# Gate rows split into single jobs, a reordered opening and final norm, and projection sums laid 384 + 256 over two banks

## The chip, the cores and the metric

The kernel runs on one core of one Trainium2 chip, in one launch. The metric is device time in microseconds (us); lower is better. Five engines work side by side, each on its own queue of instructions: TensorE (PE, matmuls), VectorE (DVE), ScalarE (ACT), GpSimd (POOL) and SyncE (SP, whose queue issues nearly all transfers here).

## What is computed

Two layers over 128 context tokens and 512 latent tokens. Each layer has a mixer and a SwiGLU feed-forward part; both take a normalised input with shift and scale, and are added to x through a gate. Shift, scale and gate come from one small vector-matrix product per layer; the context tokens have a conditioning vector of their own.

```python
def rms_norm(x, g):
    return x * lax.rsqrt(jnp.mean(x * x, axis=-1, keepdims=True) + EPS) * g

for l in range(2):                       # for the context with c_ctx, for the latents with c
    sh1, sc1, g1, sh2, sc2, g2 = jnp.split(jax.nn.silu(cvec) @ w_ada[l] + b_ada[l], 6, axis=-1)
    h = rms_norm(x, norm_g[l, 0]) * (1 + sc1) + sh1
    y = even_mixer(h) if l % 2 == 0 else attention(h)    # pooling and short convolution; grouped-query attention
    x = x + g1 * y
    h = rms_norm(x, norm_g[l, 1]) * (1 + sc2) + sh2
    a, b = jnp.split(h @ w_ffn_in[l], 2, axis=-1)
    x = x + g2 * ((jax.nn.silu(a) * b) @ w_ffn_out[l])
y = rms_norm(x, final_g)
```

Here `D_MODEL` is 1024 and `D_FF` 2816. The keys and values of the context are outputs too.

## The kernel before

x stays in SBUF transposed: 128 partitions by 8 blocks of channels by 640 tokens, the context first (0 to 127), the latents behind (128 to 639). All matmuls are fp32 in accuracy: each operand is split into a high and a low half, and three products (high by high, high by low, low by high; `THREE`) are summed. The names show it: `wh_in` and `wl_in` are the halves of in-projection weights loaded as `raw_in`, `ah` and `al` those of x times the scale. The high half of a weight is made on ScalarE (L144), the low half on DVE (L145).

One output block of a projection is a PSUM tile of two banks of 512 columns; `block_mm` (L282) lays tokens 0 to 319 in the first bank and 320 to 639 in the second (`HT` is 320), so each weight is used by a pair of 320-wide matmuls. `project` runs the blocks of one projection; its `each(i)` is called ahead of block i, its `done` after it, one step late. `residual` (L515) adds a block to x with the gate: three operations through `update` (L501), for the context, for 192 latents in the first bank and for 320 in the second.

The rows of shifts, scales and gates, 96 of 128 outputs each, come from two places. The parts needed first are computed by PE at the start (`ada_pe`, `ada_row`, `ada_turn`: a product per quarter of a chunk, a copy on ScalarE, a transposition by PE). All others are computed on DVE by `AdaDve`: one row is a 512 KB transfer on SP's queue (L354), four reductions of 128 x 512 (L371) and four reads of their sums. `ada.run(n)` computes the next n rows of a list of jobs; a job (layer, first row, count) is written to `mod` only when its last row is done. The numbers in the `each` and `fast_each` arguments thus set how much of DVE's time goes to rows at which step.

The program runs in this order (times from the profile): the opening, up to 62.8 us, in an order written out by hand (`manual_schedule`); behind it a scheduler orders each engine's instructions, where the reductions of the rows stay in the order of the program. In-projection of layer 0, 13 blocks (`pi`), to 166; its output projection (`po`) to 223; the feed-forward part of layer 0 in three groups, each with its up-projection and a down-projection: group 0 has four plain blocks and, from 285, four by the fast algorithm (`fast_blocks`, which forms sums of weights on DVE, L236 to L242, and halves of the SwiGLU product in `uv`, L652 and L657), down-projection `fo0_0` 337 to 394; group 1 fast 394 to 496 and `fo0_1` to 553; group 2 to 672. Then layer 1: attention to 916, plain blocks to 965, fast blocks of group 0 to 1027, `fo1_0` to 1084, and so on, to the final norm.

The final norm (`last1`) works in two parts of 384 and 256 tokens. Sums of squares are multiplied by ones on PE (`ms_fin`), `Norm.finish` makes `rstd` in three steps on ScalarE and three on DVE (L474 to L476), and `out` (L1443) multiplies eight blocks by `rstd`, every third on GpSimd, with a transfer for each two blocks.

Of the kernel before, what the change touches and what calls it, by code (L numbers as in the profile page):

```python
# [36 lines left out]
EARLY = 30  # L37
# [23 lines left out]
def hybrid_step(  # L61
# [611 lines left out]
    def ffn(l, xin, hid, each=None, last=None, spare=None, fast_each=None):  # L673
# [37 lines left out]
        for gi, (f0, f1) in enumerate(GROUPS):  # L711
# [21 lines left out]
            if plain:  # L733
                project(f"fi{l}_{gi}", xin, KB, 2 * plain, in_done, ext=True, each=each and (lambda i: each(i, True)))
# [11 lines left out]
    with tc.tile_pool(name="pool1", bufs=1) as p1:  # L746
# [6 lines left out]
        def ada_load(ch):  # L753
# [851 lines left out]
```

## Time and profile before

| | |
|---|---|
| median of 3 runs | 1377.84 us (1377.27 to 1378.74) |
| profiled execution, its own time | 1376.99 us |
| its span | 1375.2 us |
| PE busy | 1327.7 us, 97% |
| DVE busy | 1081.2 us, 79% |
| ScalarE, GpSimd busy | 636.3 us, 70.3 us |
| mean rate of the transfers | 113 GB/s |

All rows below come from the profiled execution, whose time is 0.85 us under the median; times in them count from the start of its span. L is a line of the kernel before. In a timeline a run of like instructions stands as one row, with the start of its first, the time until its last one ends and their count; idle time ahead of it and what ended it stand in brackets. In a row of windows the columns after the length are the busy time of PE, PE's loads of weights, DVE, ScalarE and GpSimd, each with its number of instructions, then the mean granted clock of PE (1.00 is the 2.4 GHz level, 0.50 the 1.2 GHz one), the mean busy share of the 16 DMA engines and GB/s.

### The profile page before, as it was taken

To read this page: it belongs to the slowest core of one execution; us is meant where nothing else is said; L and a number is where in the kernel's file an instruction comes from. 1 tells how busy PE (TensorE), PEld (TensorE's weight loads), DVE (VectorE), ACT (ScalarE), POOL (GpSimd) and SP (SyncE) were. 2 spreads that over 40 slices of the span, in tenths; PEclk is the share of its full clock that TensorE was granted. 3 is DMA by queue.
4 is the path that set the end of the run, shared out by engine and by line. 5 is a ranking of instruction groups with operands and counts; after the bars stand their busy time and mean duration, and the time that the engine had idled before them with its cause. 6 is when DMAs were issued, how large, how long until landed. Compare 5 with 4: busy or idle time off the path is not lost.

```text
span 1375.2 us, 22538 instructions
## 1 busy us (share of the span) xinstructions
PE 1327.7 (97%) x8929; PEld 1294.1 (94%) x8929; DVE 1081.2 (79%) x2182; ACT 636.3 (46%) x1155; POOL 70.3 (5%) x73
## 2 busy tenths in 40 slices
PE   6989999989999999999999999999999999999995
PEld 3889999989999999999998899999999999999995
DVE  4899988999988898789976777689993577446745
ACT  3532335744135531454565675477551255314543
POOL 3200000000000000000013121000000000000013
PEclk7999999999999999999999999999999999999998
DMA  9635523134533254324531110031242122311212
GB/s 363 250 117 176 195 93 123 64 106 169 172 123 114 95 187 154 108 92 140 188 95 55 43 49 34 32 134 53 106 154 77 62 76 78 123 62 62 77 47 77
DMA packets 36872, 155.54 MB, mean 113 GB/s; under 512 B 4000, under 2 KB 11168, under 8 KB 26016
## 3 DMA queue, kind: packets, MB, share of 16 engines
q1 hardware_dynamic: 36768, 154.12, 32.2%
q8 instruction: 70, 1.15, 0.3%
q14 instruction: 34, 0.28, 0.1%
HBM read 148.60 MB, written 2.88 MB: 110 GB/s over the span
## 4 chain that ended last, share of the span: by engine, by line
PE 77%; DVE 16%; ACT 3%; issue 2%; DMA 1%; SPq 0%; POOL 0%; DVEq 0%; ACTq 0%; POOLq 0%
PE fi L630 24%; PE fo L289 21%; PE fi L289 7%; PE pq L289 5%; PE pi L289 5%; DVE junk L371 5%; PE po L289 4%; DVE wl_fi_p L145 3%; PE wb L289 2%; PE wa L289 2%; PE o L1326 2%; PE s L1276 1%; PE t L1309 1%; ACT wh_fi_p L144 1%; DMA raw_ada<-wada 1%
## 5 line engine op out<-in xcount | busy, mean ns | idle before, releaser
L144 ACT ACTIVATE wh_fi_p<-raw_fi 128x512 fp32r<-128x512 f32 x252 | 153.9, 626 | 219.5 <-PE fi L630 108.6
L371 DVE CUSTOM_DVE_ANT_0 junk<-rawa,silb 128x512 f32<-128x512 f32 x336 | 237.0, 705 | 6.5 <-DMA rawa<-wada 2.2
L145 DVE TENSOR_TENSOR wl_fi_p<-raw_fi,wh_fi_p 128x512 fp32r<-128x512 f32 x252 | 170.1, 686 | 64.1 <-ACT wh_fi_p L144 63.9
L506 DVE SCALAR_TENSOR_TENSOR x<-fo,mod,x 128x128 f32<-128x128 f32 (+1 forms) x144 | 55.5, 433 | 94.1 <-PE fo L289 90.8
L144 ACT ACTIVATE wh_fo<-raw_fo 128x1024 fp32r<-128x1024 f32 (+1 forms) x48 | 47.5, 990 | 145.4 <-PE fo L289 121.2
L630 PE MATMUL fi<-bh,wh_fi_p 128*128 128x320 f32 x288 | 89.0, 309 | 0.7 <-DVE x L506 0.5
L630 PE MATMUL fi<-bh,wl_fi_p 128*128 128x320 f32 x288 | 88.9, 309 | 0.6 <-DVE wl_fi_p L145 0.6
L630 PE MATMUL fi<-ah,wl_fi_p 128*128 128x320 f32 x288 | 88.8, 308 | 0.0
L630 PE MATMUL fi<-al,wh_fi_p 128*128 128x320 f32 x288 | 88.7, 308 | 0.0
L630 PE MATMUL fi<-ah,wh_fi_p 128*128 128x320 f32 x288 | 88.4, 307 | 0.0
L630 PE MATMUL fi<-bl,wh_fi_p 128*128 128x320 f32 x288 | 88.4, 307 | 0.0
L289 PE MATMUL fo<-al,wh_fo 128*128 128x320 f32 x352 | 80.8, 310 | 0.0
L289 PE MATMUL fo<-ah,wh_fo 128*128 128x320 f32 x352 | 80.6, 310 | 0.1
L289 PE MATMUL fo<-ah,wl_fo 128*128 128x320 f32 x352 | 80.4, 309 | 0.0
L289 PE MATMUL fo<-bh,wh_fo 128*128 128x320 f32 x328 | 75.2, 310 | 0.0
L289 PE MATMUL fo<-bh,wl_fo 128*128 128x320 f32 x328 | 75.0, 310 | 0.0
L289 PE MATMUL fo<-bl,wh_fo 128*128 128x320 f32 x328 | 74.9, 310 | 0.0
L630 PE MATMUL fi<-x0h,wh_fi_p 128*128 128x320 f32 x216 | 69.0, 323 | 5.0 <-DVE uv L652 3.6
L630 PE MATMUL fi<-xh,wh_fi_p 128*128 128x320 f32 x216 | 68.0, 320 | 2.6 <-DVE uv L652 2.1
L630 PE MATMUL fi<-x0l,wh_fi_p 128*128 128x320 f32 x216 | 66.9, 311 | 0.0
L630 PE MATMUL fi<-x0h,wl_fi_p 128*128 128x320 f32 x216 | 66.9, 311 | 0.0
L289 PE MATMUL pi<-ah,wh_in 128*128 128x320 f32 (+1 forms) x256 | 62.3, 326 | 4.7 <-ACT ev L526 3.8
(375 smaller groups left out, 3808.7 us busy)
## 6 DMA issues: line engine op xcount, KB each, us to landing
raw_fi<-wfi SPq DMA_DIRECT2D x44, 1024.0 KB, 4.8
rawa<-wada SPq DMA_DIRECT2D x84, 512.0 KB, 3.4
raw_fo<-wfo SPq DMA_DIRECT2D x16, 1024.0 KB, 4.9
raw_ada<-wada SPq DMA_DIRECT2D x12, 512.0 KB, 9.9
raw_in<-win SPq DMA_DIRECT2D x6, 1024.0 KB, 6.4
raw_fo<-wfo SPq DMA_DIRECT2D x8, 768.0 KB, 4.2
raw_qkv<-wqkv SPq DMA_DIRECT2D x6, 1024.0 KB, 5.0
raw_out<-wout SPq DMA_DIRECT2D x4, 1024.0 KB, 4.8
```

Of the source, the lines that this page charges most:

```text
L144: S.activation(h, src, AF.Copy)
L145: eng.tensor_tensor(out=l, in0=src, in1=h.bitcast(F32), op=ALU.subtract)
L289: PE.matmul(ps[:, h, 0 : hi - lo], w[a][:, k, cols], rhs[b][:, k0 + k, lo:hi], start=k == 0 and a == b, stop=k == kn - 1 and a == 1,)
L371: op = V.tensor_tensor_reduce(out=self.junk, in0=raw[:, cols], in1=self.silb[:, c, cols], scale=1.0, scalar=0.0, op0=ALU.mult, op1=ALU.add ...
L506: V.scalar_tensor_tensor(out=xs, in0=got[:, 0 : b - a], scalar=mod[l][:, gate0 + m, c : c + 1], in1=xs, op0=ALU.mult, op1=ALU.add,)
L630: PE.matmul(out, w[a][:, k, :], ops.get(OPERAND[p], b)[:, k, :], start=fresh and k == 0 and a == b, stop=k == ops.kn - 1 and a == 1, skip_ ...
L1276: PE.matmul(self.ps[:, hf, 0:HT], bufB[a][:, self.h, q0 : q0 + P], kt[b][:, self.kv, hf * HT : hf * HT + HT], start=n == 0, stop=n == 2,)
L1309: PE.transpose(flat(pt)[:, s * P : s * P + P], self.pe[:, s * P : s * P + P], ident)
L1326: PE.matmul(po[:, 0 : 2 * P], vt[a][:, self.kv, s * P : s * P + P], got[b][:, s, :], start=s == 0 and n == 0, stop=s == 4 and n == 2,)
```

## The change

- **Layout.** Sums for `po`, `fo`, `wa` and `wb` (all that go into x) are cut at token 384 instead of 320 (`CUT`). All latents then lie as 256 columns in each bank, and one operation of 128 x 2 x 256 updates them; the context has one of its own. The in-projections keep 320.
- **Gate rows.** The feed-forward gates of both layers are eight jobs of one row each, so that a residual needs its own gate row alone. Rows that DVE computes move: the opening keeps 4; `pi` has 16 instead of 18 (per step 1,1,1,1,1,2,2,2,1,1,1,1,1 instead of 2,2,2,2,2,2,2,1,1,1,1,0,0); `po` and the two blocks ahead of it keep theirs; the plain blocks of layer 0 have 0 instead of 3, its fast blocks 0, 8 and 6 in the three groups instead of 4, 4 and 3, its down-projections 12, 14 and 8 instead of 12, 12 and 8. In layer 1 eight rows go from the fast blocks of group 0 to `fo1_0`, one a step; the transfers of the first two start at the head of the stage.
- **Opening.** The first weights are loaded ahead of chunk 3; 6, 3 and 14 matmuls on zeros are put in (`turn_over`); the transposition of chunk 2 no longer stands behind a part of chunk 3; squares of x move from GpSimd to ScalarE and their sums to DVE; the order of splits and matmuls changes.
- **Final norm.** The first part's `finish` gets a high priority; the multiplications by `rstd` are four operations of four blocks each on DVE, none on GpSimd, with four transfers instead of eight. In DVE's order the second part's finish still stands behind both of the first part's operations.

```diff
-EARLY = 30
+EARLY = 28
...
-    def block_mm(ps, w, rhs, kn, ext=False, mcol=0, k0=0, ks=None):
+    CUT = CTX + LAT // 2
+
+    def block_mm(ps, w, rhs, kn, ext=False, mcol=0, k0=0, ks=None, cut=HT):
...
-        span = ((0, 0, HT), (1, HT, TX if ext else T))
+        span = ((0, 0, cut), (1, cut, TX if ext else T))
...
     def residual(ps, m, l, gate0):
-        parts = ((0, 0, CTX, ps[:, 0]), (1, CTX, HT, ps[:, 0, CTX:]), (1, HT, T, ps[:, 1]))
-        update(m, l, gate0, parts)
+        update(m, l, gate0, [(0, 0, CTX, ps[:, 0])])
+        xs = halves(x[:, m, CTX:T])
+        V.scalar_tensor_tensor(
+            out=xs,
+            in0=flat(ps)[:, CTX : CTX + 768].rearrange("p (a b) -> p a b", a=2)[:, :, 0 : LAT // 2],
+            scalar=mod[l][:, gate0 + m, 1:2],
+            in1=xs,
+            op0=ALU.mult,
+            op1=ALU.add,
+        )
...
-            [(0, 4, 4)] + [(0, 8 * p, 8) for p in (2, 4, 3, 5)] + [(1, 8 * p, 8) for p in (1, 0, 2, 4, 3)]
+            [(0, 4, 4)]
+            + [(0, 8 * p, 8) for p in (2, 4, 3)]
+            + [(0, 40 + b, 1) for b in range(8)]
+            + [(1, 8 * p, 8) for p in (1, 0, 2, 4, 3)]
...
+        ws.load(1, cut=True)
         ada_load(3)
-        ws.load(1, cut=True)
...
+        idle = first[2][:, 0, :]
+
+        def turn_over(n):
+
+            for _ in range(n):
+                PE.matmul(idle, zeror, zeror2, start=True, stop=True)
+
+        turn_over(6)
         acc = {ch: ada_acc(ch) for ch in (2, 3)}
         ada_pe(2, acc[2], range(4))
         row = ada_row(2, acc[2])
-        ada_pe(3, acc[3], range(1))
+        turn_over(3)
         ada_turn(2, row)
-        ada_pe(3, acc[3], range(1, 4))
+        turn_over(14)
         for k in range(4):
-            nrm.add(k, pool_only=True)
-        prep(0, bufA, 0, 0)
-        prep(1, bufA, 0, 0)
-        prep(2, bufA, 0, 0)
-        ws.split(0, ahead=False)
+            prep(k, bufA, 0, 0)
+            if k == 1:
+                ws.split(0, ahead=False)
+        ws.split(1, ahead=False)
+        for k in range(4):
+            nrm.square(k)
+        first_mm(0, range(4))
+        ada_pe(3, acc[3], range(4))
         row = ada_row(3, acc[3])
-        prep(3, bufA, 0, 0)
-        ws.split(1, ahead=False)
-        first_mm(0, range(0, 2))
+        nrm.add_square(V)
...
+        first_mm(1, range(2))
         ada_turn(3, row)
-        first_mm(0, range(2, 4))
-        first_mm(1, range(4))
+        first_mm(1, range(2, 4))
...
-        ada.run(2, hold=False)
+        ada.run(1, hold=False)
+        nrm.add_square(V)
...
+        ada.run(1, hold=False)
...
-            each=lambda i: ada.run(1 + (i < 7) - (i >= 11)),
+            each=lambda i: ada.run(1 + (5 <= i < 8)),
...
-                each=lambda i, plain=False: ada.run(int(i >= 5) if plain else 1 + i % 2),
-                fast_each=lambda gi, n, p: ada.run(int(p == 6 and (gi == 0 or n % 2))),
+                each=lambda i, gi, plain=False: ada.run(0 if plain else 1 + (i % 2 if gi == 0 else int(i > 1))),
+                fast_each=lambda gi, n, p: ada.run(int(p == 6 and gi > 0)),
...
-                (G if k % 3 == 1 else V).tensor_tensor(out=xs, in0=xs, in1=rstd[:, cols], op=ALU.mult)
...
+            V.tensor_tensor(
+                out=xs, in0=xs, in1=rstd[:, None, cols].broadcast_to((P, ks.stop - ks.start, n)), op=ALU.mult
+            )
+            nc.sync.dma_start(yT[:, ks, cols], xs)
...
-            nrm.finish((lo, hi), None)
+            with tc.high_priority():
+                nrm.finish((lo, hi), None)
...
-    gates = AdaDve([(1, 40, 8)], 76)
+    gates = AdaDve([(1, 40 + b, 1) for b in range(8)], 76)
     gates.home(p3, p3, 2, ps_small("junk1"), silb)
+    gates.load()
+    gates.load()
...
-        fast_each=lambda gi, n, p: gates.run(int(gi == 0 and p in (1, 6))),
+        each=lambda i, gi, plain=False: gates.run(0 if plain or gi else 1),
```

How instructions move is shown at three places. On PE in the opening, before (`adap` is a product of a chunk, one row of two matmuls a quarter, `adat` the transposition, `pi_152` the first block of the in-projection):

```order
L306 MATMUL adap_155<-raw_ada_3_103,silc 2x512 x2
L306 MATMUL adap_157<-raw_ada_0_107,silc 2x512 x2
L330 MATMUL adat_171<-kc,row_167 128x2 x4
L306 MATMUL adap_157<-raw_ada_1_109,silc 2x512 x2
L306 MATMUL adap_157<-raw_ada_2_111,silc 2x512 x2
L306 MATMUL adap_157<-raw_ada_3_113,silc 2x512 x2
L289 MATMUL pi_152<-ah,wh_in_0_204 128x320 x2
L289 MATMUL pi_152<-al,wh_in_0_204 128x320 x2
L289 MATMUL pi_152<-ah,wl_in_0_205 128x320 x2
```

and after:

```order
L309 MATMUL adap_161<-raw_ada_3_103,silc 2x512 x2
L827 MATMUL pi_154<-zeror 128x512 x3
L333 MATMUL adat_178<-kc,row_173 128x2 x4
L827 MATMUL pi_154<-zeror 128x512 x14
L292 MATMUL pi_152<-ah,wh_in_0_207 128x320 x2
L292 MATMUL pi_152<-al,wh_in_0_207 128x320 x2
L292 MATMUL pi_152<-ah,wl_in_0_208 128x320 x2
```

The transposition of chunk 2 stood behind a quarter of chunk 3; now matmuls on zeros (`pi_154<-zeror`) stand around it, and all of chunk 3 comes after the first block's matmuls with the first half of x.

On DVE in the in-projection, before, around one of the scaled projections `ev` (`pl` is a pooling result, `junk,got` a reduction of a row, `got` alone the read of its sum):

```order
L915 SCALAR_TENSOR_TENSOR pl_747<-s_4_588,up_578 128x128
L371 ISA junk,got_16_591<-rawa_371,silb 128x512
L371 ISA got_16_591 128x1
L915 SCALAR_TENSOR_TENSOR pl_747<-s_4_588,up_578 128x512
L371 ISA junk,got_16_591<-rawa_371,silb 128x512
L371 ISA got_16_591 128x1
L521 TENSOR_TENSOR ev_754<-pi_676,rstd 128x640
L371 ISA junk,got_16_591<-rawa_379,silb 128x512
L371 ISA got_16_591 128x1
L145 TENSOR_TENSOR bl<-pl_747,bh 128x640
```

and after:

```order
L956 SCALAR_TENSOR_TENSOR pl_760<-s_4_613,up_603 128x128
L956 SCALAR_TENSOR_TENSOR pl_760<-s_4_613,up_603 128x512
L534 TENSOR_TENSOR ev_767<-pi_695,rstd 128x640
L374 ISA junk,got_16_616<-rawa_396,silb 128x512
L374 ISA got_16_616 128x1
L145 TENSOR_TENSOR bl<-pl_760,bh 128x640
L374 ISA junk,got_16_616<-rawa_396,silb 128x512
L374 ISA got_16_616 128x1
```

Two reductions, and their reads, have left the place between `pl` and `ev`.

On DVE where the second down-projection of layer 0 passes into the third group's fast blocks, before (`fo_1_7` is the last block, `wl_fi_16_p` and on are low halves of the fast blocks' weights):

```order
L506 SCALAR_TENSOR_TENSOR x<-fo_1_7_5294,mod_77,x 128x128
L371 ISA junk,got_32_5162<-rawa_5241,silb 128x512
L371 ISA got_32_5162 128x1
L506 SCALAR_TENSOR_TENSOR x<-fo_1_7_5294,mod_77,x 128x192
L371 ISA junk,got_32_5162<-rawa_5241,silb 128x512
L371 ISA got_32_5162 128x1
L506 SCALAR_TENSOR_TENSOR x<-fo_1_7_5294,mod_77,x 128x320
L145 TENSOR_TENSOR wl_fi_16_p_5400<-raw_fi_16_4964,wh_fi_16_p_5399 128x512
L145 TENSOR_TENSOR wl_fi_16_p_5400<-raw_fi_17_5096,wh_fi_16_p_5399 128x512
L236 TENSOR_TENSOR raw_fi_17_5096<-raw_fi_17_5096 128x4x128
```

and after:

```order
L509 SCALAR_TENSOR_TENSOR x<-fo_1_7_5298,mod_77,x 128x128
L374 ISA junk,got_32_5307<-rawa_5246,silb 128x512
L374 ISA got_32_5307 128x1
L523 SCALAR_TENSOR_TENSOR x<-fo_1_7_5298,mod_77,x 128x512
L374 ISA junk,got_32_5307<-rawa_5246,silb 128x512
L374 ISA got_32_5307 128x1
L145 TENSOR_TENSOR wl_fi_16_p_5404<-raw_fi_16_4953,wh_fi_16_p_5403 128x512
L374 ISA junk,got_32_5307<-rawa_5246,silb 128x512
L374 ISA got_32_5307 128x1
L145 TENSOR_TENSOR wl_fi_16_p_5404<-raw_fi_17_5092,wh_fi_16_p_5403 128x512
L374 ISA junk,got_32_5307<-rawa_5246,silb 128x512
L374 ISA got_32_5307 128x1
```

The update of x has one operation less, and reductions now stand between the update and the low halves as well as between these; before, the first ones behind the update came after thirteen other instructions.

## Rows read from the trace of the kernel before

**Rows 1.** The page: busy time by engine; the chain that ended last.

```profile
PE 1327.7 (97%) x8929; PEld 1294.1 (94%) x8929; DVE 1081.2 (79%) x2182; ACT 636.3 (46%) x1155; POOL 70.3 (5%) x73
...
PE 77%; DVE 16%; ACT 3%; issue 2%; DMA 1%; SPq 0%; POOL 0%; DVEq 0%; ACTq 0%; POOLq 0%
```

**Rows 2.** Waits of PE: line, released by, total us, times, longest us.

```profile
PE fi L630 <- DVE uv L652: 5.8, 3, 3.6
PE pi L289 <- DVE wl_in L145: 4.7, 3, 3.4
PE pi L289 <- ACT ev L526: 3.8, 1, 3.8
```

**Rows 3.** Windows: from:to, length, busy us by engine (x instructions), clock, DMA.

```profile
26.00:28.00 2.00, 1.87 (x7) 1.87 (x8) 2.00 (x4) 0.00 (x0) 0.00 (x0) 0.50 1.02 410
75.00:100.00 25.00, 21.24 (x125) 20.79 (x123) 25.00 (x65) 9.00 (x15) 0.33 (x6) 0.86 0.31 106
285.00:300.00 15.00, 10.59 (x60) 9.82 (x59) 15.00 (x33) 5.36 (x11) 0.00 (x0) 0.89 0.26 81
400.00:625.00 225.00, 223.10 (x1490) 218.21 (x1490) 191.56 (x384) 93.34 (x178) 0.00 (x0) 1.00 0.36 123
500.00:550.00 50.00, 50.00 (x340) 50.00 (x339) 45.15 (x113) 7.73 (x9) 0.00 (x0) 1.00 0.47 158
975.00:1025.00 50.00, 47.52 (x318) 46.15 (x318) 50.00 (x114) 24.75 (x47) 0.00 (x0) 1.00 0.37 127
1025.00:1075.00 50.00, 50.00 (x341) 49.96 (x340) 22.26 (x37) 9.37 (x12) 0.00 (x0) 1.00 0.30 106
```

**Rows 4.** Timeline of the start: start us, us, engine, line, operands, xcount [idle].

```profile
10.68 0.60 ACT L324 ACTIVATE row<-adap 98x512 f32<-98x512 f32 x1 [7.79 <-PE adap L306]
...
13.16 1.25 POOL L436 TENSOR_TENSOR ssq_a<-x 128x640 f32<-128x640 f32 x1 [11.27 <-DMA x<-xT]
...
14.43 1.03 PE L306 MATMUL adap<-raw_ada,silc 128*2 128x512 f32 x4 [3.80 <-DMA raw_ada<-wada]
...
17.73 7.21 DVE L485 SCALAR_TENSOR_TENSOR al<-x,sc,ah 128x128 fp32r<-128x128 f32 x6 [0.47 <-ACT ah L483]
...
24.86 1.21 DVE L145 TENSOR_TENSOR wl_in<-raw_in,wh_in 128x1024 fp32r<-128x1024 f32 x1
...
26.13 0.90 PE L289 MATMUL pi<-ah,wl_in 128*128 128x320 f32 x2 [3.42 <-DVE wl_in L145]
...
36.89 8.03 POOL L440 TENSOR_TENSOR ssq_a<-ssq_a,sq_a 128x640 f32<-128x640 f32 x4 [13.42 <-ACT sq_a L438]
...
37.61 1.94 DVE L371 CUSTOM_DVE_ANT_0 junk<-rawa,silb 128x512 f32<-128x512 f32 x1
...
54.14 0.48 DVE L474 SCALAR_TENSOR_TENSOR ssq_a<-ms_a,ssq_a 128x320 f32<-128x320 f32 x1
```

**Rows 5.** The page's costliest groups: xcount | busy us, mean ns | idle before.

```profile
L371 DVE CUSTOM_DVE_ANT_0 junk<-rawa,silb 128x512 f32<-128x512 f32 x336 | 237.0, 705 | 6.5 <-DMA rawa<-wada 2.2
```

**Rows 6.** Timeline, layer 0's second down-projection: one residual's three updates.

```profile
524.60 1.13 DVE L506 SCALAR_TENSOR_TENSOR x<-fo,mod,x 128x128 f32<-128x128 f32 x3
```

**Rows 7.** Chain of waits, layer 0's first down-projection: start us, us, what.

```profile
337.54 56.54 PE fo L289 x384
```

**Rows 8.** Timeline of PE near the end: matmuls of 384 and 256 columns.

```profile
1348.51 0.34 PE L1461 MATMUL fo<-bh,wh_fo 128*128 128x384 f32 x1
...
1354.80 0.28 PE L1461 MATMUL fo<-bh,wh_fo 128*128 128x256 f32 x1
...
1356.81 0.28 PE L1461 MATMUL fo<-bh,wl_fo 128*128 128x256 f32 x1
```

**Rows 9.** Timeline of the tail: final normalisation on DVE.

```profile
1362.17 4.83 DVE L1446 TENSOR_TENSOR x<-x,rstd 128x384 f32<-128x384 f32 x5
...
1366.92 0.41 DVE L474 SCALAR_TENSOR_TENSOR ssq_fin<-ms_fin,ssq_fin 128x256 f32<-128x256 f32 x1
...
1368.15 3.35 DVE L1446 TENSOR_TENSOR x<-x,rstd 128x256 f32<-128x256 f32 x5
```

More of the change, by code (lines that the diff above doesn't have):

```diff
@@ L501, in update @@
     def update(m, l, gate0, parts):
-        assert (l, gate0 // 8, 8) in known
+        assert any((l, gate0 // 8, n) in known for n in range(m + 1, 9))
         for c, a, b, got in parts:
@@ L559, in project @@
                 each(i)
-            pipe.step(lambda: block_mm(ps, w, rhs, kn, ext=ext), lambda: done(i, ps))
+            pipe.step(lambda: block_mm(ps, w, rhs, kn, ext=ext, cut=cut), lambda: done(i, ps))
     def updater(l, gate0, nrm, then):
@@ L733, in ffn @@
             if plain:
-                project(f"fi{l}_{gi}", xin, KB, 2 * plain, in_done, ext=True, each=each and (lambda i: each(i, True)))
+                project(f"fi{l}_{gi}", xin, KB, 2 * plain, in_done, ext=True, each=each and (lambda i: each(i, gi, True)))
             if l in FAST:
@@ L739, in ffn @@
             if gi < len(GROUPS) - 1:
-                project(f"fo{l}_{gi}", hid, f1 - f0, KB, lambda k, ps: residual(ps, k, l, 40), each=each)
+                project(
+                    f"fo{l}_{gi}",
+                    hid,
+                    f1 - f0,
+                    KB,
+                    lambda k, ps: residual(ps, k, l, 40),
+                    each=each and (lambda i: each(i, gi)),
+                )
             else:
@@ L1415, in hybrid_step @@
         for m in range(2):
-            pipe.step(lambda: block_mm(fw[m], wpart[0], bufB, 4, mcol=m, k0=4, ks=range(3)))
+            pipe.step(lambda: block_mm(fw[m], wpart[0], bufB, 4, mcol=m, k0=4, ks=range(3), cut=CUT))
         assert not pipe.due
@@ L1419, in hybrid_step @@
         for m in range(2):
-            pipe.step(lambda: block_mm(fw[m], wpart[0], bufB, 4, mcol=m, k0=4, ks=(3,)), lambda: out_done(m, fw[m]))
+            pipe.step(lambda: block_mm(fw[m], wpart[0], bufB, 4, mcol=m, k0=4, ks=(3,), cut=CUT), lambda: out_done(m, fw[m]))
         for m in range(2, KB):
@@ L1441, in whole, with out @@
             gain(k)
-        def out(cols, step):
-            for k in range(KB):
-                xs = x[:, k, cols]
-                (G if k % 3 == 1 else V).tensor_tensor(out=xs, in0=xs, in1=rstd[:, cols], op=ALU.mult)
-                if k % step == step - 1:
-                    ks = slice(k + 1 - step, k + 1)
-                    nc.sync.dma_start(yT[:, ks, cols], x[:, ks, cols])
+        def out(ks, cols):
+            n = cols.stop - cols.start
+            xs = x[:, ks, cols]
+            V.tensor_tensor(
+                out=xs, in0=xs, in1=rstd[:, None, cols].broadcast_to((P, ks.stop - ks.start, n)), op=ALU.mult
+            )
+            nc.sync.dma_start(yT[:, ks, cols], xs)
         project("fo1_2", bufA, kn, KB - 2, whole)
@@ L1470, in last1 @@
                 nrm.add(KB - 2 + m, V, cols)
-            nrm.finish((lo, hi), None)
+            with tc.high_priority():
+                nrm.finish((lo, hi), None)
             for m in range(2):
                 gain(KB - 2 + m, cols)
-        for h, (lo, hi) in enumerate(spans):
-            out(slice(lo, hi), 2)
+            if not h:
+                out(slice(0, 4), cols)
+        for h, ks in ((0, slice(4, 8)), (1, slice(0, 4)), (1, slice(4, 8))):
+            out(ks, slice(*spans[h]))
     whole_b = tuple(t.rearrange("p a b -> p (a b)") for t in bufB)
```

18 lines of the change are left out of this document (13 added, 5 removed).

## The prediction

> **What bounds the kernel now.** I read the page first: TensorE (PE) is busy for 1327.7 of 1375.2 us, 97%, and the chain that ended last runs through PE for 77% and through VectorE (DVE) for 16% of the span [rows 1]. So at most some 47 us stand idle, and work taken off DVE pays only where PE waits for it. Next I read what PE waited for [rows 2]: the two halves of a SwiGLU product (`uv`), the low halves of the in-projection's weights (`wl_in`) and one scaled projection (`ev`). Each of these hangs on an instruction in DVE's queue. Then the windows around these waits [rows 3]. In 75 to 100 us DVE is busy for all 25.00 us and PE has 125 matmuls; a matmul costs 147 ns at full speed (below), so 170 would fit and 6.6 us are lost, part of it as a gap, part since the granted clock averages 0.86 there: PE waited and then ran some 7 us at the 1.2 GHz level. In 285 to 300 DVE is again busy throughout, 60 matmuls stand where 100 would fit: 6.0 us lost, at a mean clock of 0.89. In 975 to 1025, DVE at 50.00 of 50, PE is idle for 2.5 us and the clock stays at 1.00. In 500 to 550 DVE is at 90% and PE never stops. So a full DVE stalls PE and a DVE at 90% does not; the change takes rows (`AdaDve.run`, four reductions each) out of three full places and puts them into emptier ones.
>
> **The start, -5.5 us (3 to 7).** The first matmul that needs a low half waits 3.42 us, until 26.13, for `wl_in`, which DVE starts only at 24.86 [rows 4]. Two things delay it. PE stands 3.80 us for the fourth-part transfers of chunk 3 and runs them from 14.43, while the transposition of chunk 2, whose input ScalarE has ready at 10.68 + 0.60 = 11.28, is queued behind; the change puts it ahead, and the first scaling can start when x is there, which GpSimd reads from 13.16: some 3.5 us earlier. And DVE's six `al` operations from 17.73 take 7.21 us beside GpSimd's squares; after the change ScalarE squares and only four `al` precede `wl_in`. Worked through, `wl_in` starts at 17 to 18 instead of 24.86, its limit being ScalarE's `wh_in` behind four `ah`. Much of the 7 us is lost again: PE runs these matmuls at the 1.2 GHz level (clock 0.50 in 26 to 28, [rows 3]), the second half of x comes behind the same transfers, and chunk 3 lands later since the first weights now pass it on SP's queue. The second place is the row reductions: one takes 1.94 us from 37.61 while GpSimd's additions run from 36.89 for 8.03 us [rows 4], against 0.705 on average over all 336. Four such lose 4 x 1.23 = 4.9 us on DVE, on the path to the third block's `wl_in` and the norm's step at 54.14. The change puts the additions on DVE itself: a 320-wide two-input operation takes 0.48 and a 256-wide 0.41 [rows 4, 9], so 1.1 ns a column and 0.13 fixed, 0.83 for 640 columns; four cost 3.3 back, and this gives 1.6; three more stand ahead of the second `al` and are covered by PE's queue of matmuls. I get the step at 54.14 to 47.5 to 51 and take 5.5; 3 if the transfers set it, 7 if everything shifts. The extra matmuls on zeros lie where PE was idle; whether they hold the 2.4 GHz level no row shows, so I count no gain. Fourteen of 512 columns, at twice the 0.147 us per 320, take 6.6 us and would end near 19, a loss of 1 to 2 that the 3 contains; at the fast level they end before `wl_in`.
>
> **The in-projection, -5.0 (3 to 6.6).** Five of the first five steps' rows go and three come back later, net two. A row is 4 x 0.705 = 2.8 us [rows 5], taken as 3.0 with the reads of its four sums, so 15 us of DVE leave ahead of the gap in 75 to 100, which should close it and the slow clock behind it: 6.6 at most. But the rows that come back land in a stage where DVE has little room, so over the whole stage only the two rows' 6 us are free. I take 5.0.
>
> **First fast blocks of layer 0, -5.5 (4 to 6).** Four rows leave these blocks and three the plain ones ahead: 20.6 us of DVE in a place that lost 6.0. The wait for `uv` of 3.6 us [rows 2] goes with them; late next would be ScalarE, whose busy time there is 5.36 of 15. **First fast blocks of layer 1, -2.0 (1.2 to 2.4):** eight rows leave, the loss was 2.5. They go into the down-projection behind, where DVE has 22.26 of 50 [rows 3]; seven rows make it 43, below the 90% that cost nothing. The fourteen added small additions (each less than the 0.41 us of a 256-wide operation) lie in the same slack and in that of layer 0's first down-projection; a residual waits for its own gate alone, on one queue.
>
> **The rows put into layer 0's later blocks, +4 (0 to +9).** Nine rows, 27 us, enter 400 to 625, where DVE has 191.56 of 225 [rows 3]: 218.6, or 97%. At 90% the cost was nothing. At 100% it was 2.5 in 50 us, and 225 such us would lose 11.2, less the 1.9 that are idle there already: 9.3. 97% lies nearer the full end, but the place is full only by count and not in arrears; two rows a step, in the second down-projection, make 2 x 3.0 + 1.2 for the split of weights (1.21 for 1024 columns, [rows 4]) + 1.0 for the updates = 8.2 us of DVE in a step of 7.07, and the overhang slides into the next blocks, as the order shows. I take 4. Their transfers, 512 KB each on SP's queue, enter windows with DMA at 0.36.
>
> **The 384 and 256 layout, -2.0 (0 to 2.7).** The updates of one residual take 1.13 us [rows 6]; two operations instead of three save one fixed part. At 1.1 ns a column 640 columns are 0.70, so the fixed part is 0.14, and 70 residuals save 10 us of DVE, nearly all beside matmuls: nothing on the path. That an operation across two banks costs more, no row shows; at twice the 0.7 for 512 columns it would take 49 us more of DVE, in stages with room but for the second down-projection. For PE: 384 matmuls of 320 columns take 56.54 us, 147.2 ns each and 294.5 a pair [rows 7]. The 384-wide ones go 36 in 1354.80 - 1348.51 = 6.29 us, 174.7 ns, the 256-wide 17 in 1356.81 - 1354.80 = 2.01, 118.2 [rows 8]: 292.9 a pair, 1.6 less, and there are 1404 pairs: 2.3. Runs of like size are not alternation, which no row shows; I take 2.0.
>
> A rule speaks against this term. The Trainium skill ("TensorE: Matmul & The Clock Gate", section "Back-to-back issue gap") states for the isolated gap N/2.4 + 2.5 ns, a straight line through which 320 + 320 and 384 + 256 cost the same 271.7 ns; by it the term is 0. The trace does not agree with its figure: 147.2 ns, not 135.8, for 320 columns.
>
> **The tail, -1.5 (0.5 to 2.5).** From 1362.17 five multiplications of 384 columns take 4.83 us beside GpSimd's three, and only then, at 1366.92, does DVE finish the second half's norm; from 1368.15 five more take 3.35 [rows 9]. In the changed order that finish still stands behind both wide operations. Two of 1536 columns, by the slope and fixed part above, take 3.6, so 1.2 is saved, and two of 1024 take 2.5, 0.8 saved. The last transfer is 512 KB instead of 256, which gives some back: 1.5 of 2.0 are left.
>
> **Sum.** -5.5 - 5.0 - 5.5 - 2.0 + 4 - 2.0 - 1.5 = -17.5. The profiled execution took 1376.99 (span 1375.2), 0.85 under the median: 1359.5 profiled, 1360.3 as median.
>
> **Rivals.** (1) The moved rows stall PE: 1360.3 + 5.3 = 1365.6. For it: 97%; against it: 90% costs nothing. Chance 0.18. (2) The start gives 2 instead of 5.5, since transfers or the slow clock set it: 1363.8. For it: the transfers were the wait at 14.43. Chance 0.12. (3) The layout gives PE nothing, a straight line in the columns: 1362.3. Chance 0.05, for the rows 8 were taken on like sizes. (4) Slower: a 256-wide matmul behind a 384-wide one cannot hide the load of its weights and takes 147.2 as a 320-wide does: 174.7 + 147.2 = 321.9 a pair, 27.4 more, 1404 x 27.4 = 38.5 us, 1362.3 + 38.5 = 1400.8. It decides from (1377.84 - 1362.3) / 1404 = 11.1 ns a pair. Against it: seventeen 256-wide matmuls, each with its own load, ran at 118 ns. Chance 0.03. The forecast itself has 0.60; 0.02 is for what I don't see.
>
> **Range and chances.** All good ends together give 1350.6, all bad ones 1375.4; neither is likely whole, and 1350 to 1370 holds (1) to (3). A difference of 0.2% (2.8 us) is about what can be told from none. Faster 0.95: all but (4) and a pile of bad ends; same 0.02; slower 0.03.
>
> **What would show it.** Right: `wl_in` near 18 us and the norm's step below 51; no wait for `ev` near 85 and the clock at 1.00 there; no wait for `uv` of over 1 us; a down-projection of 384 matmuls at 56.2 us or less; 11.5 us from the first wide multiplication to the end, where it was 1375.2 - 1362.17 = 13.0. Wrong: PE waits for DVE summing to over 6 us in 390 to 630, DVE at 100% there; a pair over 306 ns; the step at 54.14 later than 52.

## The result, and the profile of the changed kernel

The changed kernel takes 1358.30 us (median of 4 runs, 1357.14 to 1358.87) where the kernel before takes 1377.55 in the same comparison (1377.21 to 1378.74): a ratio of 0.9858, 95% interval 0.9841 to 0.9875. That is 19.25 us, 1.4% faster; the forecast was 1360.3. The profiled execution has a span of 1356.7 us, 18.5 less than the one before.

The page, as in [rows 1]: busy time, then the chain that ended last, by engine.

```profile
PE 1328.0 (98%) x8952; PEld 1296.2 (96%) x8952; DVE 1075.4 (79%) x2141; ACT 638.5 (47%) x1159; POOL 46.3 (3%) x56
...
PE 82%; DVE 11%; ACT 3%; issue 2%; DMA 1%; SPq 0%; POOL 0%; DVEq 0%; ACTq 0%; POOLq 0%
```

PE does the same work, 23 matmuls on zeros more, in a shorter span, and DVE's part of the chain fell from 16% to 11%. PE's waits, as in [rows 2] (line, released by, total us, times, longest):

```profile
PE pi L292 <- DVE wl_in L145: 2.2, 2, 1.8
...
PE pi L292 <- ACT ev L539: 1.9, 1, 1.9
...
PE fi L644 <- DVE x L523: 0.2, 1, 0.2
PE fi L644 <- DVE uv L666: 0.2, 1, 0.2
```

The waits for `uv` are gone (5.8 to 0.2 us); those for `wl_in` and `ev` are about halved. Up to the last matmul two stretches of slow clock are left, from 40.5 to 47.3 and from 81.4 to 84.8 us, the first around a wait for `wl_in`, the second behind the wait for `ev`. Windows as in [rows 3]:

```profile
40.00:44.00 4.00, 2.41 (x11) 2.41 (x11) 3.90 (x10) 2.14 (x5) 0.00 (x0) 0.56 1.03 413
60.00:80.00 20.00, 19.00 (x128) 18.73 (x126) 20.00 (x46) 8.01 (x13) 0.41 (x8) 1.00 0.32 105
80.00:84.00 4.00, 3.07 (x13) 3.07 (x14) 4.00 (x11) 0.82 (x2) 0.10 (x3) 0.68 0.06 19
285.00:321.00 36.00, 35.98 (x242) 35.07 (x242) 26.22 (x41) 19.17 (x36) 0.00 (x0) 1.00 0.26 88
380.00:605.00 225.00, 223.26 (x1490) 218.19 (x1489) 211.04 (x448) 93.47 (x178) 0.00 (x0) 1.00 0.42 143
960.00:1010.00 50.00, 49.61 (x334) 48.43 (x333) 37.42 (x59) 25.62 (x51) 0.00 (x0) 1.00 0.26 87
1010.00:1060.00 50.00, 50.00 (x341) 50.00 (x340) 38.44 (x96) 8.93 (x11) 0.00 (x0) 1.00 0.41 146
```

In the fast blocks of both layers' first groups (the windows from 285 and from 960) PE now stands idle for 0.02 and 0.39 us, with DVE at 73% and 75%. The window of 225 us that took the rows in has DVE at 211.04 (94%) where it had 191.56, and the same 1490 matmuls.

Read along PE's stages, from one first matmul to the next; the first `po` matmuls, before and after:

```profile
166.08 0.46 PE L289 MATMUL po<-bh,wh_out 128*128 128x320 f32 x2
...
156.61 0.46 PE L292 MATMUL po<-bh,wh_out 128*128 128x384 f32 x2
```

| stage | before, us | after, us | difference |
|---|---|---|---|
| opening and in-projection, to the first `po` matmul | 166.08 | 156.61 | -9.47 |
| `po` | 56.65 | 56.67 | 0.0 |
| layer 0, up-projection of group 0 | 114.65 | 107.97 | -6.7 |
| layer 0, from its first down-projection on | 335.13 | 335.53 | +0.4 |
| attention and its output projections | 243.92 | 244.74 | +0.8 |
| layer 1, up-projection of group 0 | 110.68 | 108.37 | -2.3 |
| layer 1, from `fo1_0` to the last sum of the norm | 335.20 | 335.39 | +0.2 |
| last sum to the end | 12.91 | 11.46 | -1.5 |

The +0.8 of the attention is not explained: there PE waits 1.1 us for one low half (`pt_2l`) where it waited 0.5, and the kernels below that keep the new layout take 243.8 to 245.0 us for this stage.

The timeline of the opening, as in [rows 4]:

```profile
10.24 0.60 ACT L327 ACTIVATE row<-adap 98x512 f32<-98x512 f32 x1 [7.26 <-PE adap L309]
...
13.78 1.68 DVE L488 SCALAR_TENSOR_TENSOR al<-x,sc,ah 128x512 fp32r<-128x512 f32 x3 [0.27 <-ACT ah L486]
15.63 1.23 DVE L145 TENSOR_TENSOR wl_in<-raw_in,wh_in 128x1024 fp32r<-128x1024 f32 x1 [0.17 <-ACT wh_in L144]
...
33.98 3.61 DVE L431 TENSOR_TENSOR ssq_a<-ssq_a,sq_a 128x640 f32<-128x640 f32 x4
...
47.60 0.48 DVE L477 SCALAR_TENSOR_TENSOR ssq_a<-ms_a,ssq_a 128x320 f32<-128x320 f32 x1
```

The first low half starts at 15.63 instead of 24.86 and the norm's step (the first of its three on DVE, the last row above) at 47.60 instead of 54.14. The tail, as in [rows 9]:

```profile
1345.14 3.42 DVE L1487 TENSOR_TENSOR x<-x,rstd 128x1536 f32<-128x1536 f32 x2
...
1348.48 0.42 DVE L477 SCALAR_TENSOR_TENSOR ssq_fin<-ms_fin,ssq_fin 128x256 f32<-128x256 f32 x1
...
1349.72 2.36 DVE L1487 TENSOR_TENSOR x<-x,rstd 128x1024 f32<-128x1024 f32 x2
```

### The profile page after: what moved, and what is told of

Read it like the earlier page. It is cut to its first block, busy times and chain, and to the rows that moved or that the text cites. A ratio compares the mean times of both kernels' runs of the same rounds, so it can differ in the third digit from the quotient of the medians.

```text
span 1356.7 us, 22528 instructions
## 1 busy us (share of the span) xinstructions
PE 1328.0 (98%) x8952; PEld 1296.2 (96%) x8952; DVE 1075.4 (79%) x2141; ACT 638.5 (47%) x1159; POOL 46.3 (3%) x56
## 4 chain that ended last, share of the span: by engine, by line
PE 82%; DVE 11%; ACT 3%; issue 2%; DMA 1%; SPq 0%; POOL 0%; DVEq 0%; ACTq 0%; POOLq 0%
PE fi L644 28%; PE fo L292 19%; PE fi L292 8%; PE pi L292 6%; PE pq L292 5%; PE po L292 4%; DVE junk L374 4%; PE wb L292 2%; PE wa L292 2%; PE o L1367 2%; PE s L1317 2%; DVE wl_fi_p L145 1%; PE t L1350 1%; ACT wh_fi_p L144 1%; DMA x<-xT 1%
## 5 line engine op out<-in xcount | busy, mean ns | idle before, releaser
L374 DVE CUSTOM_DVE_ANT_0 junk<-rawa,silb 128x512 f32<-128x512 f32 x336 | 232.7, 692 | 6.4 <-DMA rawa<-wada 1.2
L144 ACT ACTIVATE wh_fo<-raw_fo 128x1024 fp32r<-128x1024 f32 (+1 forms) x48 | 47.5, 990 | 147.9 <-PE fo L292 129.5
L292 PE MATMUL fo<-al,wh_fo 128*128 128x384 f32 (+1 forms) x352 | 81.0, 311 | 0.0
L292 PE MATMUL fo<-ah,wh_fo 128*128 128x384 f32 x352 | 80.8, 311 | 0.1
L292 PE MATMUL fo<-ah,wl_fo 128*128 128x384 f32 x352 | 80.5, 310 | 0.0
L509 DVE SCALAR_TENSOR_TENSOR x<-fo,mod,x 128x128 f32<-128x128 f32 (+1 forms) x52 | 18.5, 359 | 73.3 <-PE fo L292 69.8
L292 PE MATMUL fo<-bh,wh_fo 128*128 128x384 f32 x328 | 75.2, 310 | 0.0
L292 PE MATMUL fo<-bh,wl_fo 128*128 128x384 f32 (+1 forms) x328 | 75.1, 310 | 0.0
L292 PE MATMUL fo<-bl,wh_fo 128*128 128x384 f32 x328 | 75.0, 310 | 0.0
L644 PE MATMUL fi<-xl,wh_fi_p 128*128 128x320 f32 x216 | 66.5, 309 | 0.0
L644 PE MATMUL fi<-xh,wl_fi_p 128*128 128x320 f32 x216 | 66.5, 309 | 0.0
```

The costliest lines, as they stand in the source:

```text
L144: S.activation(h, src, AF.Copy)
L292: PE.matmul(ps[:, h, 0 : hi - lo], w[a][:, k, cols], rhs[b][:, k0 + k, lo:hi], start=k == 0 and a == b, stop=k == kn - 1 and a == 1,)
L374: op = V.tensor_tensor_reduce(out=self.junk, in0=raw[:, cols], in1=self.silb[:, c, cols], scale=1.0, scalar=0.0, op0=ALU.mult, op1=ALU.add ...
L509: V.scalar_tensor_tensor(out=xs, in0=got[:, 0 : b - a], scalar=mod[l][:, gate0 + m, c : c + 1], in1=xs, op0=ALU.mult, op1=ALU.add,)
L644: PE.matmul(out, w[a][:, k, :], ops.get(OPERAND[p], b)[:, k, :], start=fresh and k == 0 and a == b, stop=k == ops.kn - 1 and a == 1, skip_ ...
```

## The experiments

The theory from the two traces: the gain comes from three things on DVE, namely no GpSimd beside it in the opening, no gate rows ahead of the places where PE waits for it, and the shorter tail; the layout gives nothing. Each kernel below was timed beside the kernel before on the same chip, where that one has a median of 1377.24 to 1377.64 us; times are medians. Each is profiled once. How far a single profile can be trusted is seen where kernels have the same code: in the seven with the changed kernel's opening the norm's step comes at 47.4 to 48.1, and in the four that share its in-projection too the first `po` matmul comes at 155.6 to 157.5, so a share read there holds to about 1 us.

### The layout undone

```diff
-    CUT = CTX + LAT // 2
+    CUT = HT
...
-        update(m, l, gate0, [(0, 0, CTX, ps[:, 0])])
...
+        parts = ((0, 0, CTX, ps[:, 0]), (1, CTX, HT, ps[:, 0, CTX:]), (1, HT, T, ps[:, 1]))
+        update(m, l, gate0, parts)
```

> The changed kernel with its layout alone undone: all sums laid 320 + 320, each residual in three DVE operations again. Theory A (the pair of 384 + 256 costs PE what 320 + 320 costs, and DVE's 70 x 0.13 us lie beside matmuls): 1358.3 us within 1.5, the 384 matmuls of a down-projection at 56.5 to 56.9 us. Theory B (the term of the prediction): 2.0 slower, 1360.3, since each of 1404 pairs gets 1.4 ns longer. Theory C (the cheaper update is what lets DVE carry the rows moved into layer 0's later blocks): 1361 to 1364, with waits of PE for DVE of 3 to 6 us between 380 and 540.

1358.94 us (1358.67 to 1359.18): no difference that can be told. The chain of waits shows layer 0's and layer 1's first down-projections (start, us, what), first of the changed kernel:

```profile
321.41 56.89 PE fo L292 x384
...
1010.05 56.67 PE fo L292 x384
```

and with 320 + 320:

```profile
322.31 56.54 PE fo L292 x384
...
1010.03 56.63 PE fo L292 x384
```

So 384 matmuls take 56.7 to 56.9 us in pairs of 384 + 256 (295.2 ns a pair in layer 1) and 56.5 to 56.6 in equal pairs (294.9). Theory B falls: a pair is not 1.4 ns shorter, and the term of -2.0 is zero. Of theory C a piece is right. Where the second down-projection of layer 0 passes into the next fast blocks, PE waits once more in the kernel with 320 + 320:

```profile
PE fi L636 <- DVE x L509: 1.9, 1, 1.9
```

In the changed kernel this wait is 0.2 us. The update is cheaper there as forecast: the second operation starts 0.27 us after the first and the next instruction 0.65 after that, 0.92 in all, where the three took 1.05 (524.60 to 525.65 in the timeline of before).

```profile
501.84 0.35 DVE L509 SCALAR_TENSOR_TENSOR x<-fo,mod,x 128x128 f32<-128x128 f32 x1
502.11 0.74 DVE L523 SCALAR_TENSOR_TENSOR x<-fo,mod,x 128x512 f32<-128x512 f32 x1
...
502.76 0.69 DVE L374 CUSTOM_DVE_ANT_0 junk<-rawa,silb 128x512 f32<-128x512 f32 x1
```

In these two profiles larger differences by stage offset each other. In layer 0, from its first down-projection on, the kernel with 320 + 320 takes 336.7 us against 335.5; in the attention it takes 243.0 against 244.7. Why the attention is shorter is open.

### The plan of gate rows undone

```diff
-EARLY = 28
+EARLY = 30
...
-            each=lambda i: ada.run(1 + (5 <= i < 8)),
+            each=lambda i: ada.run(1 + (i < 7) - (i >= 11)),
...
-                each=lambda i, gi, plain=False: ada.run(0 if plain else 1 + (i % 2 if gi == 0 else int(i > 1))),
-                fast_each=lambda gi, n, p: ada.run(int(p == 6 and gi > 0)),
+                each=lambda i, gi, plain=False: ada.run(int(i >= 5) if plain else 1 + i % 2),
+                fast_each=lambda gi, n, p: ada.run(int(p == 6 and (gi == 0 or n % 2))),
...
-        each=lambda i, gi, plain=False: gates.run(0 if plain or gi else 1),
+        fast_each=lambda gi, n, p: gates.run(int(gi == 0 and p in (1, 6))),
```

The lists of jobs go back with them, and in layer 1 the two early transfers.

> The changed kernel with the plan of gate rows alone undone (30 early rows, the steps' counts of before, gates as one job of eight, layer 1's gates in its first fast blocks). Theory A (the rows are what closed the stalls of three places, 2.9 + 6.7 + 2.3 us between the two traces): 1358.3 + 12 = 1370, range 1367 to 1372, with PE's waits for uv (5 to 6 us) and for ev (3 to 4 us) back. Theory B (part of the gain in the in-projection came from the opening, which hands over earlier): the ev wait stays below 2 us and the time is 1366 to 1368.

1371.39 us (1370.85 to 1371.90), 13.1 slower than the changed kernel: theory A, with the waits of before for `uv` and `ev` back to the tenth.

```profile
PE fi L644 <- DVE uv L666: 5.8, 3, 3.6
...
PE pi L292 <- ACT ev L539: 3.8, 1, 3.8
```

By stages: 4.5 us to the first `po` matmul (161.16 against 156.61), of which 0.5 are a later opening (norm's step at 48.09), 6.9 in layer 0's up-projection of group 0, 2.5 in layer 1's. This also parts the first stage of the table: with the rows of before the new opening alone brings the first `po` matmul from 166.08 to 161.16, 4.9 us.

### The matmuls on zeros left out

```diff
-        turn_over(6)
...
-        turn_over(3)
...
-        turn_over(14)
```

> The changed kernel without the 23 matmuls on zeros in the opening; the accumulators' own two stay. Theory A (they keep TensorE at the 2.4 GHz level through the opening): the granted clock falls to 0.50 for some microseconds after 12 us, the first halves of the first two blocks take up to 5 us longer, and of that 1 to 4 us reach the end: 1359.5 to 1362. Theory B (the opening is set by transfers and DVE, the zeros fill idle time only): 1358.3 within 1.5, the norm's step at 47.6 within 0.5 whatever the clock shows.

1359.00 us (1357.67 to 1359.73): theory B for the time. Theory A is right on the clock alone. PE stood nearly idle from 12 to 16 us, and the windows (here PE's busy time, granted clock, DMA share and GB/s) show the 1.2 GHz level until shortly before 20:

```profile
12.00:14.00 2.00, 0.09 (x1) 0.71 1.16 307
14.00:16.00 2.00, 0.28 (x1) 0.50 1.13 334
16.00:18.00 2.00, 2.00 (x8) 0.50 1.01 404
18.00:20.00 2.00, 2.00 (x10) 0.58 1.06 422
20.00:22.00 2.00, 2.00 (x18) 1.00 1.06 438
```

With the zeros the same stretch is at 1.00. The norm's step comes at 48.43 instead of 47.60, outside the 0.5 us that theory B allowed; kernels with one and the same opening show it at 47.4 to 48.1, so that most of the 0.8 us need not be the clock's. The first `po` matmul starts at 156.78 instead of 156.61.

### The sums of squares back on GpSimd

```diff
-            nrm.square(k)
+            nrm.add(k, pool_only=True)
...
-        nrm.add_square(V)
...
-            nrm.square(k)
+            nrm.add(k)
```

> The changed kernel's opening with the sums of squares back on GpSimd (first four squares on GpSimd too), all else as changed. Theory A (DVE's reductions and low halves slow down beside GpSimd's two-input operations): the al operations and four or more row reductions stretch to 1.2 to 2 us again, DVE's norm step moves from 47.6 to 51 to 53 us, and the time is 1361 to 1364. Theory B (DVE does the same work for itself in the same time): norm step within 1 us of 47.6 and 1358.3 within 1.5.

1366.50 us (1366.41 to 1367.31), 8.2 slower: theory A, and more than it expected. The timeline of the opening:

```profile
18.71 2.55 DVE L145 TENSOR_TENSOR wl_in<-raw_in,wh_in 128x1024 fp32r<-128x1024 f32 x1
...
39.28 1.93 DVE L374 CUSTOM_DVE_ANT_0 junk<-rawa,silb 128x512 f32<-128x512 f32 x1
...
55.73 0.48 DVE L477 SCALAR_TENSOR_TENSOR ssq_a<-ms_a,ssq_a 128x320 f32<-128x320 f32 x1
```

The low half takes 2.55 us instead of 1.23 and four reductions 1.9 instead of 0.69; PE waits 5.1 us for `wl_in`. The norm's step comes at 55.73, later than in the kernel before (54.14): at this place the new order without the moved sums is a loss.

### The sums moved in the kernel before, and nothing else

```diff
-        for k in range(4):
-            nrm.add(k, pool_only=True)
...
+        for k in range(4):
+            nrm.square(k)
+        for k in range(4):
+            nrm.add_square(V)
...
-            nrm.add(k)
+            nrm.square(k)
...
-        ada.run(2, hold=False)
+        ada.run(1, hold=False)
+        for k in range(4):
+            nrm.add_square(V)
+        ada.run(1, hold=False)
```

> The kernel before with one part of the change alone: the opening's squares on ScalarE and their sums on DVE, its order, transfers and rows left as they are. Theory A (GpSimd beside DVE is what the opening lost): the six al operations take 3.3 instead of 7.2 us, no reduction over 0.8 us, the norm's step at 49 to 51 instead of 54.1, 1373 to 1374.5. Theory B (the early transposition and the transfers' order are the larger half): norm step at 52 to 53, 1375.5 to 1377.

1373.80 us against 1377.24, a ratio of 0.9974 (0.9965 to 0.9983): theory A.

```profile
18.43 2.60 DVE L485 SCALAR_TENSOR_TENSOR al<-x,sc,ah 128x512 fp32r<-128x512 f32 x5 [0.26 <-ACT ah L483]
...
49.79 0.48 DVE L474 SCALAR_TENSOR_TENSOR ssq_a<-ms_a,ssq_a 128x320 f32<-128x320 f32 x1
...
161.72 0.46 PE L289 MATMUL po<-bh,wh_out 128*128 128x320 f32 x2
```

The six `al` operations end 3.2 us after their start (17.82 to 21.03) and the norm's step moves by 4.35. So the sums give 4.35 of the 6.5 us at the norm's step, and the new order 2.2 more on top of them, but only with them. At the first `po` matmul the sums alone give 4.4 us (166.08 to 161.72), where the whole new opening with the old rows gives 4.9: what is left there of the new order, 0.6 us, lies within the noise.

### More rows where rows were put

```diff
-                fast_each=lambda gi, n, p: ada.run(int(p == 6 and gi > 0)),
+                fast_each=lambda gi, n, p: ada.run(int((p == 6 and gi > 0) or (p == 1 and gi == 1 and n % 2))),
```

> The changed kernel with four more gate rows in the second group's fast blocks of layer 0 (12 rows in eight blocks instead of 8); the four last rows of the group behind fall away there, since the list ends earlier. It asks where the moved rows begin to cost. DVE's need over these 101 us rises from about 94% by 12 us to 105%. Theory A (it costs nothing until the time is full, then what exceeds it): PE waits for DVE or ScalarE of 3 to 8 us between 378 and 480, 1361 to 1366. Theory B (rows are deferred behind the weights' halves and the excess is taken up by the down-projection and the blocks behind): 1358.3 within 1.5, no wait over 1 us. Theory C (the price of the prediction, 9.3 us per 225 at a full DVE, so 4 per 100): 1362.

1357.24 us (1356.33 to 1361.10): theory B. The window of those blocks:

```profile
380.00:480.00 100.00, 99.86 (x670) 97.73 (x670) 99.39 (x220) 52.35 (x100) 0.00 (x0) 1.00 0.46 156
```

DVE is busy for 99.39 of 100 us and PE for 99.86. Theories A and C fall: with a full DVE nothing stalls here. Theory B's reason is not what the trace shows: hardly anything is put off, for 51 reductions start inside these blocks where 36 did, so that 15 of the 16 added ones fit. From its first down-projection on, layer 0 takes 334.7 us here, 335.5 in the changed kernel. Of this profile's lead of 2.4 us, 1.0 comes from the in-projection, whose rows are the changed kernel's: PE waits the same 1.9 us for `ev`, but the clock stays at 1.00 behind it, and the first `po` matmul starts at 155.62 instead of 156.61.

```profile
PE pi L292 <- ACT ev L539: 1.9, 1, 1.9
...
80.00:84.00 4.00, 2.52 (x17) 2.52 (x18) 4.00 (x9) 1.29 (x3) 0.17 (x3) 1.00 0.18 71
```

### Rows of the in-projection put off

```diff
-            each=lambda i: ada.run(1 + (5 <= i < 8)),
+            each=lambda i: ada.run(0 if i < 3 else 1 + (i >= 7)),
```

> The changed kernel with the in-projection's 16 rows later: none in the first three steps, one in the next four, two in the last six. Theory A (only the place matters: the wait for ev at 78.6 and the slow clock behind it, 1.9 + 2.2 us, come from the three rows ahead of it): 1354 to 1355.5, no wait for ev, clock 1.00 throughout 60 to 100. Theory B (DVE is the bound over the whole stage, 94.7 of 97 us busy, and every row put off comes back as a wait later): the wait moves to 100 to 160, a wait for wl_in or ev of 2 to 5 us, 1357 to 1361.

1355.47 us (1354.44 to 1358.75). One row alone, from the first step to the ninth, with the first piece of the output cut in two:

```diff
-            each=lambda i: ada.run(1 + (5 <= i < 8)),
+            each=lambda i: ada.run(1 - (i < 1) + (5 <= i < 9)),
...
-                out(slice(0, 4), cols)
+                out(slice(0, 2), cols)
+                out(slice(2, 4), cols)
```

> The changed kernel with one row of the in-projection put off from the first step to the ninth, and the first piece of the output cut in two so that its transfer starts 0.8 us earlier. Theory A (3.0 us of DVE less ahead of the wait for ev close its 1.9 us and the slow clock behind): 1354 to 1355, of which the tail gives 0.3 to 0.8. Theory B (DVE is the bound of the stage): 1357 to 1358, the gap comes later.

1354.72 us (1354.14 to 1354.95; ratio to before 0.9834, 0.9819 to 0.9849), 3.6 faster than the changed kernel; the tail has 0.4 of it (11.1 us instead of 11.5 from the last sum's matmul to the end), the in-projection nearly all the rest. Theory A in both. Windows of the one with three steps free:

```profile
60.00:100.00 40.00, 40.00 (x271) 40.00 (x270) 39.17 (x75) 15.88 (x26) 0.85 (x15) 1.00 0.30 106
100.00:157.00 57.00, 57.00 (x385) 57.00 (x384) 56.36 (x132) 17.88 (x28) 0.17 (x3) 1.00 0.53 185
157.00:213.00 56.00, 55.90 (x379) 55.66 (x378) 55.30 (x131) 23.03 (x34) 0.00 (x0) 1.00 0.35 117
```

and of the other:

```profile
60.00:80.00 20.00, 19.98 (x134) 19.71 (x134) 19.80 (x43) 8.86 (x14) 0.52 (x9) 1.00 0.25 83
80.00:100.00 20.00, 20.00 (x137) 20.00 (x136) 19.67 (x40) 7.09 (x12) 0.33 (x6) 1.00 0.38 124
```

PE hardly stops, the clock stays at 1.00, and DVE is at 98 to 99% all the way. Part of the rows put off went into the output projection behind: 40 reductions start there instead of 33 (37 with the one row), and where DVE is busy for 55.30 of 56 us the changed kernel has 52.10:

```profile
157.00:213.00 56.00, 56.00 (x382) 56.00 (x381) 52.10 (x122) 20.55 (x31) 0.00 (x0) 1.00 0.32 111
```

What stalled PE was three rows ahead of one instruction, where two do not, and not the stage's load.

### The end undone

```diff
-            V.tensor_tensor(
-                out=xs, in0=xs, in1=rstd[:, None, cols].broadcast_to((P, ks.stop - ks.start, n)), op=ALU.mult
-            )
...
+                (G if k % 3 == 1 else V).tensor_tensor(out=xs, in0=xs, in1=rstd[:, cols], op=ALU.mult)
...
-            with tc.high_priority():
-                nrm.finish((lo, hi), None)
+            nrm.finish((lo, hi), None)
```

> The changed kernel with its end alone undone: sixteen multiplications by rstd shared with GpSimd, eight transfers. Theory A (DVE alone does the same columns sooner, the prediction's 1.5): 1359.8, the five DVE multiplications of the first part at 4.8 us instead of 3.4 for the two wide ones, 12.9 us instead of 11.4 from the last sum's matmul to the end. Theory B (the transfers' rate sets the end, whatever DVE does): 1358.3 within 0.7 and the end 11.4 to 12 us behind that matmul.

1359.35 us (1358.61 to 1360.27): the span is 1.4 longer (1358.1 against 1356.7) and 12.9 us lie between the last sum's matmul, at 1345.24, and its end, where 11.5 lie in the changed kernel. The five multiplications are back at their old length:

```profile
1345.11 4.82 DVE L1487 TENSOR_TENSOR x<-x,rstd 128x384 f32<-128x384 f32 x5
```

Theory A by the trace; the medians' 1.05 us alone would not tell it from noise.

### The third block's weights earlier

On top of the one row put off:

```diff
+        ws.load(2, cut=True)
         ada_load(0)
-        ws.load(2, cut=True)
...
-        ada.run(1, hold=False)
         ws.split(2, ahead=False)
-        ada.run(2, hold=False)
+        ada.run(3, hold=False)
```

> The kernel with one row of the in-projection put off and the first piece of the output cut in two (1354.7 us), and besides the third block's weights loaded ahead of the chunk in front of them and their low half ahead of the second row of reductions. Theory A (PE's wait of 2.2 us for this low half and the slow clock from 41 to 47 us reach the end): no such wait, clock 1.00 throughout the opening, 1351.5 to 1353.5. Theory B (DVE's queue up to the norm's step sets the opening's end): the wait goes, the norm step stays at 47.4 within 0.5, 1354.7 within 1.

1354.21 us (1353.70 to 1354.94), 0.5 less, not to be told from 1354.72. The clock in 40 to 48 is at 1.00 now, the wait for `wl_in` is down to 0.4 us, and the norm's step stays where it was (a window, then a row of the timeline):

```profile
44.00:48.00 4.00, 2.11 (x15) 1.84 (x13) 3.79 (x13) 0.00 (x0) 0.00 (x0) 1.00 1.04 410
```

```profile
47.52 0.48 DVE L477 SCALAR_TENSOR_TENSOR ssq_a<-ms_a,ssq_a 128x320 f32<-128x320 f32 x1
```

Theory B: PE now waits 2.0 us at the norm instead, where it waited 1.0. From 31 us to the norm's step DVE's queue runs without a gap, and it sets the step. The first `po` matmul starts at 152.47, against 153.18 with the one row put off alone. This is the fastest kernel of the study, at a ratio of 0.9828 (0.9814 to 0.9842) to the kernel before.

## Why the prediction was right, and where not

The time, the direction and five of the seven terms hold, one of the five (the in-projection) with a wrong limit. Two terms were wrong in what they rest on, by -3.6 and +2.0 us, and partly cancel, so that it is in part luck that the sum is only 2 us off.

| term | forecast | measured | from |
|---|---|---|---|
| opening | -5.5 (3 to 7) | -4.9 | first `po` matmul with the old rows |
| in-projection's rows | -5.0 (3 to 6.6) | -4.0 to -4.5 | the same place, against the changed kernel |
| first fast blocks, layer 0 | -5.5 (4 to 6) | -6.7 | stages; -6.9 by undoing |
| first fast blocks, layer 1 | -2.0 (1.2 to 2.4) | -2.3 | stages; -2.5 by undoing |
| rows put into later blocks | +4 (0 to 9) | +0.4 | stages |
| 384 + 256 | -2.0 (0 to 2.7) | 0 | undoing; 295.2 against 294.9 ns a pair |
| tail | -1.5 (0.5 to 2.5) | -1.5 | stages; -1.4 by undoing |

**The opening** gave about what was forecast. `wl_in` starts at 15.6, earlier than the 17 to 18 worked out; the step at 54.14 came to 47.6, at the early end of 47.5 to 51. What the prediction did not see is that 1.1 us of the 6.0 won at the norm's step (with the old rows, 54.14 to 48.09) are given back before the `po` matmuls. A new slow-clock stretch at 40 to 47 us, where PE runs out of work before the third block's low half is ready, may have part in it: without it (the last experiment) the first `po` matmul is 0.7 us earlier, within the noise. Of the two causes that the prediction named, the one that carries the term is GpSimd beside DVE, with 4.4 of the 4.9 us; that the earlier transposition and transfers are worth anything at the `po` matmuls is not shown. The zeros, counted at nothing, are worth nothing that can be told, though they do hold the clock.

**The row that stalls.** For the in-projection the mechanism was right and its limit was put in the wrong place. Five rows taken out ahead of the gap were to close it and the slow clock behind it; 1.9 of the 3.8 us of waiting for `ev` stayed, and 3.4 of the 6.8 us at the 1.2 GHz level, so that this sign of being right failed. And I let the whole stage's DVE time cap the gain, where the two runs that put rows off show there is no such cap: some 3 us more were to be had with the same number of rows (first `po` matmul at 153.18 instead of 156.61 with one row put off). In layer 0's fast blocks the loss read off one window of 15 us was 6.0; the stage held 0.7 more outside it. (Seven rows at 3.0 us are 21.0, not the 20.6 written there; nothing hangs on it.)

**The moved rows** are the step that failed. I priced a busy share: nothing at 90%, 9.3 us at 100%, so 4 at 97%. The share came out at 94%, and at 99.4%, with four rows more, the price is still nothing. So the 2.5 us that layer 1's blocks lost at 100% were no measure of a busy share. What cost them stays open. Two rows a block stood there ahead of what PE waited for; but in the run with twelve rows every second block has two rows at the same two places and PE does not wait, so that alone is not enough, and nothing tells it apart from there being more work than time. Rival (1) is out by the same run.

The price also hangs on the layout, which the prediction counted by itself. Layer 0 from its first down-projection on takes 335.1 us with the old rows and the old layout, 335.6 with the new layout alone, 336.7 with the new rows alone and 335.5 with both; seven kernels with both take 335.5 to 336.0. So the rows cost about 1.5 us without the cheaper update and nothing with it.

**The layout** is the other. The two lengths were taken from runs of like size, 174.7 and 118.2 ns; laid in turn, 384 + 256 costs 295.2 ns, as much as 320 + 320, and not their sum of 292.9. So the sign of 56.2 us or less for 384 matmuls failed too. Rival (3), the two pairs at one price, is what happened. The Trainium skill ("TensorE: Matmul & The Clock Gate", section "Back-to-back issue gap") gives a straight line in the columns for the isolated gap. The trace agrees with its form, 295.2 against 294.9 ns, and not with the estimate of 271.7 ns for a pair that follows from its figures. Rival (4) is out by far: 321.9 would have shown.

## What to carry to other kernels

Ask not how busy an engine is but what stands ahead of the instruction that the bottleneck engine waits for: here DVE at 99% cost nothing in one place, and in another putting off one job of 3 us gave 3 us, with DVE as busy as before. Before an order is tuned, take a second engine's work out from beside the one that is waited for: here that gave 4.4 of the opening's 4.9 us, and without it the new order brought the norm's step later. Costs measured on runs of equal operations need not add up when the operations alternate.

## What the runs showed of the hardware

Beside GpSimd's additions DVE's operations with two inputs in SBUF take two to three times as long: a 128 x 512 reduction 1.9 us instead of 0.69, and a 128 x 1024 subtraction 2.55 instead of 1.23. GpSimd's four additions take 8.0 us beside these reductions, DVE's own four 3.6; what GpSimd's would take with DVE idle no run shows. The Trainium skill ("SBUF — State Buffer", section "SBUF: two separate sides") describes a pair of ports that either engine holds for a whole instruction while the other is blocked; that fits the opening here, where reductions and additions last about as long as each other, 1.9 to 2.1 us.

What the slow clock cost hung here on what else set the end of the stretch. In the opening, where DVE's queue set it, PE at the 1.2 GHz level from 13 to 20 us, after standing idle, moved the norm's step by no more than 0.8 us and the first `po` matmul by 0.2. In the in-projection, after the same wait of 1.9 us for `ev`, the changed kernel had 3.4 us at that level and the one with twelve rows none, and the first `po` matmul of the latter came 1.0 us earlier.
